# A hybrid decoder trunk: forgetting attention by two pairs of heads at a time, its gates' sums added on VectorE from a table that went through memory

## The chip, the core and the metric

The kernel runs on one core of a Trainium2 chip. A core has a matrix engine (TensorE, PE in the profile, with its weight loads PEld), a vector engine (VectorE, DVE), a scalar engine (ScalarE, ACT), GpSimd (POOL) and a queue that issues transfers (SyncE, SP). Each engine works through its own instructions in the order in which they were written, and waits there for semaphores of the others. The metric is the device time of one execution in microseconds: 1077.19 us before the change, the median of three runs (1077.06 to 1077.48).

## The reference

Two layers on 256 tokens of width 1024. Each is a half-step feed-forward block, a mixer, a second half-step feed-forward block and a gated input embedding, each followed by a layer norm. The first layer's mixer is forgetting attention (FoX) with 16 heads of 64; the second layer's is latent attention. Only the first mixer is touched by the change:

```python
def fox_mixer(x, w_in, b_f, w_o):
    h = x @ w_in
    q, k, v = ...                       # 16 heads of 64 each
    f_logit = h[..., 3 * D_MODEL:] + b_f
    cum = jnp.cumsum(jax.nn.log_sigmoid(f_logit), axis=1).transpose(0, 2, 1)
    scale = FOX_HEAD_DIM ** -0.5
    def scores(start):
        ...
        s = jnp.einsum('bqhd,bkhd->bhqk', qb, k) * scale
        return s + cb[:, :, :, None] - cum[:, :, None, :]
    o = causal_block_attention(scores, v)     # causal mask, softmax, times v
    return o.reshape(B, S, D_MODEL) @ w_o
```

So to the score of query t and key s comes the difference of two running sums of log gates, cum[t] - cum[s].

## The kernel before

All matrix products run on TensorE in a float32 form that wants each operand as a high part and a low part; a product is then three matmuls (high by high, high by low, low by high: `mm3`, or three terms written out). Making the parts is the steady work of two engines: ScalarE copies the high part (line 498 for a PSUM result, lines 193 and 201 for weights), and VectorE then subtracts it from the source and writes the low part (lines 499, 194 and 205). A weight arrives by a transfer into one of three buffers `raw` (1 MB, two units each) and is split into one of ten slots `hl` or a slot that is lent for a time (`fs`, `qk`, `ota`, `otb`). `Stream.pump` decides by planned times where a split is written between matmuls; with `S.hold` set it writes none, and `S.split_now()` (or `S.ahead()` for the high part and `S.later()` for the low one) puts one at a chosen place.

The FoX mixer handles 256 tokens, eight pairs of heads j = 0..7. First come the values and gate logits (`VA`, `VB`, `VC`). `gates()` turns the logits into running sums in small steps `s1`...`s6` that are dropped between matmuls; they end in a tile `m8`, minus eight times the sums, and in `negc`, its high and low parts in four blocks of partitions. Then each pair goes through these steps, whose short names the text keeps:

- K(j) and Q(j): `gen_k`, `gen_q`, 24 matmuls of 128x256 into one bank of the PSUM ring "h" (two banks, used in turn), then the two parts into `qk` (two buffers, by j % 2).
- QK(j): for both heads the scores of the causal blocks, 384 columns, into two banks of ring "y" (four banks). Two matmuls with `sel` and `negc` put -8 cum[s] there first, and twelve matmuls of 64 rows add q by k.
- softmax(j): on VectorE four fused operations (line 1028) add the causal mask and take the row extremes, two tiny operations per head subtract and add cum[t] (`tt`, lines 1035 and 1036); on ScalarE four exponentials with row sums (line 1040); VectorE takes reciprocals (line 1047), GpSimd divides (line 1050).
- T(j): six transposes on TensorE into the two banks of ring "tr", then the parts into `PT`.
- AV(j): six matmuls, into a bank of ring "y", then the parts into `ota` or `otb` (lines 1091 and 1094).
- O(k, t): the output projection of pair k for token half t, six matmuls of 128x512 that add into two banks of ring "y".

The loop of before overlaps neighbouring pairs: K(j+1), T(j-1), QK(j), softmax(j), Q(j+1), AV(j-1). At its end come the O steps, the layer norm `ln` of each token half, and the transposes XT of the normed half that the next feed-forward block needs.

## Time and profile before

| quantity | value |
|---|---|
| time, median of 3 runs | 1077.19 us (1077.06 to 1077.48) |
| profiled execution: its time, its span | 1080.02 us, 1077.9 us |
| granted TensorE clock | 0.997 of full speed |
| TensorE busy in the span | 1064.3 us, 99% |
| VectorE, ScalarE, GpSimd busy | 721.5 us, 543.8 us, 60.2 us |
| pairs 0 to 5 of the FoX loop (223.12 to 273.56 us), busy: TensorE, VectorE, ScalarE, GpSimd | 50.44 us of 50.44; 42.08; 35.30; 14.45 |
| K(0) begins; next feed-forward block begins | 212.84 us; 305.10 us |

The profile shows one execution. A row of its timeline gives the start and the duration in us, the engine, the line, the operation with output and inputs, and in brackets the idle time of the engine just before, with what ended it. TensorE's matmuls overlap, so the time that one costs is read from start to start. A count such as x24 says that a row merges so many like instructions.

### The profile page before, as it was taken

What the parts mean: (1) busy time and instruction counts of PE and PEld (TensorE: products, weight loads), DVE (VectorE), ACT (ScalarE), POOL (GpSimd) and SP (SyncE); (2) the same over time, 40 slices, a digit from 0 to 9 for tenths busy, and PEclk for the clock granted to TensorE, in tenths of its full rate; (3) what the DMA queues carried; (4) which work ended last, traced back from release to release, by engine and by line L of the source; (5) the groups of instructions that cost most, each with busy time, mean ns of one, the idle gap of its engine ahead of it and who ended that gap; (6) DMA issues with size and microseconds to landing.
All of it is one profiled execution on the core that took longest, in us unless ns stands there. A gap on an engine that the chain in (4) does not pass through costs nothing.

```text
span 1077.9 us, 17528 instructions
## 1 busy us (share of the span) xinstructions
PE 1064.3 (99%) x7236; PEld 974.0 (90%) x7236; DVE 721.5 (67%) x1053; ACT 543.8 (50%) x805; POOL 60.2 (6%) x94
## 2 busy tenths in 40 slices
PE   9999999999999999999999999999999999999997
PEld 8989998999889899998899999988889789898986
DVE  5675545788897545548966554389877886455566
ACT  5654433667655444444564443337666465344431
POOL 0000000223100000001320000010000000000000
PEclk9999999999999999999999999999999999999999
DMA  7885642543348655444477554334334568555502
GB/s 276 335 297 222 236 159 93 204 173 118 130 177 296 233 191 196 146 177 166 168 262 274 195 194 148 108 93 147 130 126 159 185 225 314 181 207 188 186 11 78
DMA packets 33092, 199.58 MB, mean 185 GB/s; under 512 B 3699, under 2 KB 5491, under 8 KB 12149
## 3 DMA queue, kind: packets, MB, share of 16 engines
q1 hardware_dynamic: 33012, 198.47, 51.5%
q8 instruction: 57, 0.93, 0.3%
q14 instruction: 23, 0.18, 0.1%
HBM read 197.40 MB, written 1.05 MB: 184 GB/s over the span
## 4 chain that ended last, share of the span: by engine, by line
PE 87%; DVE 8%; ACT 2%; issue 1%; POOL 1%; DMA 0%; DVEq 0%; SPq 0%; POOLq 0%; ACTq 0%
PE y L489 31%; PE h L489 31%; PE tr L489 22%; DVE hl L194 2%; PE tr L493 2%; ACT P L1425 1%; DVE x L569 1%; ACT hl L193 1%; DVE PT L499 1%; DVE tr L1420 0%; DVE st L551 0%; DVE x L550 0%; PE h L493 0%; DVE qk L499 0%; DVE hl L205 0%
## 5 line engine op out<-in xcount | busy, mean ns | idle before, releaser
L194 DVE TENSOR_TENSOR hl<-raw,hl 128x1024 fp32r<-128x1024 f32 (+3 forms) x267 | 312.8, 1191 | 149.5 <-ACT hl L193 148.3
L193 ACT ACTIVATE hl<-raw 128x1024 fp32r<-128x1024 f32 (+3 forms) x267 | 269.3, 1031 | 184.9 <-PE y L489 97.6
L489 PE MATMUL y<-hl,g 128*128 128x512 f32 x816 | 190.7, 390 | 0.0
L489 PE MATMUL h<-xT,hl 128*128 128x256 f32 x1560 | 188.0, 280 | 0.4 <-DVE hl L233 0.2
L489 PEld LDWEIGHTS h<-xT,hl 128*128 128x128 f32 x1560 | 183.4, 190 | 2.6 <-ACT xT L498 0.6
L489 PEld LDWEIGHTS y<-hl,g 128*128 128x128 f32 x816 | 152.0, 188 | 30.7
L489 PE MATMUL tr<-xT,hl 128*128 128x256 f32 x1512 | 176.6, 277 | 0.0
L489 PEld LDWEIGHTS tr<-xT,hl 128*128 128x128 f32 x1512 | 174.2, 188 | 0.5
L489 PE MATMUL h<-hl,xT 128*128 128x512 f32 (+2 forms) x300 | 67.8, 374 | 0.4 <-DVE xT L499 0.4
L489 PE MATMUL y<-hl,xT 128*128 128x512 f32 (+3 forms) x360 | 65.4, 334 | 0.0
L489 PEld LDWEIGHTS h<-hl,xT 128*128 128x128 f32 x300 | 53.2, 188 | 10.7 <-DVE xT L499 1.0
L489 PEld LDWEIGHTS y<-hl,xT 128*128 128x128 f32 x360 | 55.5, 188 | 6.3 <-ACT xT L498 0.4
L561 POOL TENSOR_TENSOR rs<-ve,mhalf 128x1 f32<-128x1 f32 x16 | 15.1, 943 | 633.7 <-DVE ve L560 633.7
L489 PE MATMUL y<-hl,otb 128*128 128x512 f32 x168 | 43.8, 402 | 1.2 <-DVE otb L499 1.0
L499 DVE TENSOR_TENSOR g<-P,g 128x512 fp32r<-128x512 f32 x38 | 26.3, 693 | 26.6 <-ACT g L498 26.6
L498 ACT ACTIVATE xT<-tr 128x512 fp32r<-128x512 f32 x28 | 16.1, 597 | 49.3 <-PE tr L493 49.3
L498 ACT ACTIVATE g<-P 128x512 fp32r<-128x512 f32 x38 | 24.1, 634 | 32.7 <-DVE P L678 32.7
L489 PEld LDWEIGHTS y<-hl,otb 128*128 128x128 f32 x168 | 30.6, 192 | 7.8 <-DVE otb L499 1.4
L194 DVE TENSOR_TENSOR otb<-raw,otb 128x1024 fp32r<-128x1024 f32 (+1 forms) x20 | 24.1, 1203 | 17.3 <-ACT otb L193 17.3
L194 DVE TENSOR_TENSOR qk<-raw,qk 128x1024 fp32r<-128x1024 f32 (+1 forms) x21 | 25.7, 1222 | 12.0 <-ACT qk L193 12.0
L677 ACT ACTIVATE P<-tr 128x512 f32<-128x512 f32 x20 | 12.0, 600 | 39.3 <-PE tr L489 39.3
L678 DVE TENSOR_TENSOR P<-P,tr 128x512 f32<-128x512 f32 x20 | 13.8, 688 | 25.0 <-PE tr L489 13.4
(264 smaller groups left out, 1411.1 us busy)
## 6 DMA issues: line engine op xcount, KB each, us to landing
raw<-in_ffn_in_dram SPq DMA_DIRECT2D x85, 1024.0 KB, 4.9
raw<-in_ffn_out_dram SPq DMA_DIRECT2D x44, 1024.0 KB, 5.0
raw<-in_pg_dram SPq DMA_DIRECT2D x8, 1024.0 KB, 4.8
raw<-in_mo_dram SPq DMA_DIRECT2D x8, 1024.0 KB, 4.7
raw<-in_kq_dram SPq DMA_DIRECT2D x8, 640.0 KB, 5.2
gb<-in_ln_g_dram SPq DMA_DIRECT2D x8, 512.0 KB, 5.8
gb<-in_ln_b_dram SPq DMA_DIRECT2D x8, 512.0 KB, 7.3
raw<-in_fk_dram SPq DMA_DIRECT2D x4, 1024.0 KB, 4.9
```

Source lines behind the costliest of these rows:

```text
L193: nc.scalar.activation(hi, src, AF.Copy)
L194: nc.vector.tensor_tensor(lo, src, hi.bitcast(F32), op=ALU.subtract)
L489: self.nc.tensor.matmul(out, lhsT, rhs, start=start, stop=stop)
L493: self.nc.tensor.transpose(out, in_, self.ident)
L498: self.nc.scalar.activation(hi, src, AF.Copy)
L499: self.nc.vector.tensor_tensor(lo, src, hi.bitcast(F32), op=ALU.subtract)
L561: nc.gpsimd.tensor_tensor(rs, ve, self.mhalf, op=ALU.pow)
L569: nc.vector.scalar_tensor_tensor(xs, xs, rs if i else mv[:, 0:1], self.gb[:, i, c0:c1], op0=ALU.mult if i else ALU.subtract, op1=ALU.add i ...
L677: nc.scalar.activation(gt, ps[0], AF.Silu)
L678: nc.vector.tensor_tensor(gt, gt, ps[1], op=ALU.mult)
L1425: nc.scalar.activation(P[:, c0:c1], b[:, c0:c1], AF.Exp, bias=nm[:, q : q + 1], scale=-1.0, accum_out=su[:, q : q + 1],)
```

## The change

The running sums no longer enter the scores through TensorE. `s4` writes the 16 rows of `m8` to a small tensor `fox_c` in memory; `decay_load(j)` reads the rows of the two heads of pair j back with two transfers that repeat them on all 128 partitions, into one of two halves of a tile `mb`; `decay_mask(j)` puts the causal mask into it with two operations on GpSimd. The fused VectorE operation of softmax(j) then adds `mb` in place of the mask, and the two matmuls with `sel` and `negc` are gone from QK. Three small steps of the gates move from GpSimd to VectorE. `mb` takes the buffer of the layer norm's gains `gb`, so the gains of the mixer's norm are loaded after softmax(7) instead of at j = 2.

The loop now runs over two pairs a, a+1: QK(a), QK(a+1), softmax(a), AV(a-1), K(a+2), softmax(a+1), Q(a+2), K(a+3), T(a), Q(a+3), AV(a), T(a+1). The divisions are steps of their own (`divide`), behind softmax(a+1) and behind K(a+3). `tt` is computed for both heads of a pair at once. Four weight splits per round are written at fixed places, and AV writes into ring "h" (AV(5) into "tr"). The O steps and the last pairs are in a new order.

```diff
         bf = self.tl([128, 1], F32, "bf", 1)
-        sel = self.tl([128, 16], F32R, "sel", 1)
-        negc = self.tl([128, 384], F32R, "negc", 1)
+        mb = self.tl([128, 2, 2, 384], F32, "gb", 1)
...
-        nc.gpsimd.memset(negc.bitcast(F32), 0.0)
-        sf = fs[:, 1792:1808]
-        nc.gpsimd.tensor_tensor(sf, self.ident[:, 16:32], self.ident[:, 48:64], op=ALU.add)
-        nc.gpsimd.tensor_tensor(sf, sf, self.ident[:, 80:96], op=ALU.add)
-        nc.gpsimd.tensor_tensor(sel, sf, self.ident[:, 112:128], op=ALU.add)
...
+
+        def decay_load(j):
+
+            if not self.rec:
+                o = mb[:, j % 2]
+                for c0, n in ((0, 128), (128, 256)):
+                    row = self.fox_c[2 * j, 0:1]
+                    src = bass.AP(tensor=row.tensor, offset=row.offset, ap=[[0, 128], [256, 2], [1, n]])
+                    nc.sync.dma_start(o[:, :, c0 : c0 + n], src)
+
+        def decay_mask(j):
+
+            for c0 in (0, 256):
+                o = mb[:, j % 2, :, c0 : c0 + 128]
+                nc.gpsimd.affine_select(
+                    out=o, in_=o, pattern=[[0, 2], [-1, 128]], compare_op=ALU.is_ge, fill=NEG,
+                    base=0, channel_multiplier=1,
+                )
 
         def gates():
             ps = self.bank("tr")
@@ -930,39 +942,31 @@
                 self.S.busy(act=2400)
                 nc.gpsimd.tensor_scalar(u, e, 1.0, 1.0, op0=ALU.add, op1=ALU.mult)
                 nc.gpsimd.tensor_scalar(r, u, -1.0, 1.0, op0=ALU.add, op1=ALU.mult)
-                nc.gpsimd.tensor_tensor(e, r, e, op=ALU.subtract)
+                nc.vector.tensor_tensor(e, r, e, op=ALU.subtract)
 
             def s2():
                 nc.scalar.activation(ab, u, AF.Ln)
                 self.ready_for(AF.Exp)
                 nc.vector.reciprocal(r, u)
-                nc.gpsimd.tensor_tensor(e, e, r, op=ALU.mult)
-                nc.gpsimd.tensor_tensor(u, e, ab, op=ALU.subtract)
+                nc.vector.tensor_tensor(e, e, r, op=ALU.mult)
                 nc.gpsimd.memset(r, 0.0)
                 self.S.busy(act=1600, dve=1600)
 
             def s3():
+                nc.vector.tensor_tensor(u, e, ab, op=ALU.subtract)
                 nc.vector.scalar_tensor_tensor(f, f, 0.0, u, op0=ALU.min, op1=ALU.add)
                 nc.vector.tensor_tensor_scan(sc[fr, :], f, r, 0.0, op0=ALU.add, op1=ALU.add)
                 nc.gpsimd.tensor_scalar(m8, sc[fr, :], -8.0, 1.0, op0=ALU.mult, op1=ALU.mult)
                 self.S.busy(dve=600)
 
             def s4():
-                nc.scalar.activation(negc[fr, 0:128], m8[:, 0:128], AF.Copy)
-                nc.scalar.activation(negc[fr, 128:384], m8, AF.Copy)
-
-            def s5():
-                nc.vector.tensor_tensor(
-                    negc[64:96, 128:384], m8, negc[fr, 128:384].bitcast(F32), op=ALU.subtract
-                )
-                nc.vector.tensor_copy(negc[64:96, 0:128], negc[64:96, 128:256].bitcast(F32))
-                self.S.busy(dve=400)
-
-            def s6():
-                nc.vector.tensor_copy(negc[0:64, :], negc[64:128, :].bitcast(F32))
+                self.dma(self.fox_c, m8[16:32, :])
+                for j in range(2):
+                    decay_load(j)
+                    decay_mask(j)
 
             rest = lambda: None
-            self.bg.extend((s1, rest, rest, s2, rest, rest, s3, rest, s4, s5, s6))
+            self.bg.extend((s1, rest, rest, s2, rest, s3, s4))
 
         def gates_transpose():
...
         def gen_k(j):
-            gen(j, "fk", 256, {0: S.split_now} if j >= 2 else {}, j >= 2)
+            gen(j, "fk", 256, {}, j >= 2)
...
@@ -1000,18 +1004,12 @@
             sb = [self.bank(ring) for _ in range(2)]
             half = [slice(0, 64), slice(64, 128)]
             o = qk[:, j % 2]
-            for s in range(2):
-                h = 2 * j + s
-                self.mm(
-                    sb[s][:, 0:384], sel[half[s], h : h + 1].to_broadcast([64, 128]), negc[half[s], :],
-                    True, False,
-                )
             for n, (i, jj) in enumerate(((0, 0), (0, 1), (1, 0))):
                 for q0, c0, c1 in ((0, 0, 128), (128, 128, 384)):
                     for s in range(2):
                         self.mm(
                             sb[s][:, c0:c1], o[half[s], i, q0 : q0 + 128],
-                            o[half[s], jj, 256 : 256 + c1 - c0], False, n == 2 and q0 > 0,
+                            o[half[s], jj, 256 : 256 + c1 - c0], n == 0 and q0 == 0, n == 2 and q0 > 0,
                         )
             st[j] = sb
...
@@ -1026,14 +1024,13 @@
             for s in range(2):
                 for q, (c0, c1) in enumerate(seg):
                     nc.vector.tensor_tensor_reduce(
-                        out=sb[s][:, c0:c1], in0=sb[s][:, c0:c1], in1=self.mask[:, c0:c1],
+                        out=sb[s][:, c0:c1], in0=sb[s][:, c0:c1], in1=mb[:, j % 2, s, c0:c1],
                         op0=ALU.add, op1=ALU.min, scale=-0.125, scalar=3.0e38,
                         accum_out=nm[:, 2 * s + q : 2 * s + q + 1],
                     )
-                c2 = cq[:, 2 * j + s, :]
-                i = slice(2 * s, 2 * s + 2)
-                nc.vector.tensor_tensor(tt[:, i], nm[:, i], c2, op=ALU.subtract)
-                nc.vector.tensor_tensor(tt[:, i], tt[:, i], c2, op=ALU.add)
+            c2 = cq[:, 2 * j : 2 * j + 2, :].rearrange("p h t -> p (h t)")
+            nc.vector.tensor_tensor(tt, nm, c2, op=ALU.subtract)
+            nc.vector.tensor_tensor(tt, tt, c2, op=ALU.add)
             for s in range(2):
                 for q, (c0, c1) in enumerate(seg):
                     i = 2 * s + q
@@ -1043,17 +1040,17 @@
                     )
             self.S.busy(act=1800, dve=1400)
 
-            def divide(s):
-                nc.vector.reciprocal(su[:, 2 * s : 2 * s + 2], su[:, 2 * s : 2 * s + 2])
-                for q, (c0, c1) in enumerate(seg):
+            st[j] = P, su
+
+        def divide(j):
+            P, su = st[j]
+            nc.vector.reciprocal(su, su)
+            for s in range(2):
+                for q, (c0, c1) in enumerate(((0, 128), (128, 384))):
                     i = 2 * s + q
                     nc.gpsimd.tensor_scalar(
                         P[s][:, c0:c1], P[s][:, c0:c1], su[:, i : i + 1], 1.0, op0=ALU.mult, op1=ALU.mult
                     )
-
-            divide(0)
-            divide(1)
-            S.later()
             st[j] = P
...
-        def AV(j):
+        def AV(j, what=None):
             o = PT.pop(j)
-            ps = self.bank("y" if j < 6 else "tr")
+            ps = self.bank("h" if j != 5 else "tr")
             n, c = j // 4, 128 * (j % 4)
...
+            if what:
+                what()
             ot = OT[j // 4][:, j % 4]
...
-        for j in range(8):
-            if j == 2:
-                self.load_gb(li, 1)
-            S.hold = j >= 1
-            if j < 7:
-                gen_k(j + 1)
-            else:
-                O(0, 0)
-                O(1, 0)
-            if j == 0:
-                self.flush()
-                gates_transpose()
-                S.lend("fs")
-            if j >= 1:
-                T(j - 1)
-                if j < 7:
-                    S.ahead()
-            QK(j, "y" if j < 7 else "h")
-            softmax(j)
-            if j < 7:
-                gen_q(j + 1)
-            else:
-                O(2, 0)
-                S.split_now()
-                O(3, 0)
-            if j >= 1:
-                AV(j - 1)
+        gen_k(1)
+        gen_q(1)
+        self.flush()
+        gates_transpose()
+        S.lend("fs")
+        S.hold = True
+        for a in range(0, 8, 2):
+            QK(a, "y")
+            QK(a + 1, "y" if a < 6 else "h")
+            softmax(a)
+            if a:
+                AV(a - 1)
+            if a == 6:
+                break
+            decay_load(a + 2)
+            gen_k(a + 2)
+            softmax(a + 1)
+            decay_load(a + 3)
+            divide(a)
+            S.split_now()
+            gen_q(a + 2)
+            S.split_now()
+            gen_k(a + 3)
+            divide(a + 1)
+            decay_mask(a + 2)
+            decay_mask(a + 3)
+            T(a)
+            S.split_now()
+            gen_q(a + 3)
+            S.split_now()
+            AV(a, lambda: T(a + 1))
+        S.lend("qk")
+        O(0, 0)
+        softmax(7)
+        self.load_gb(li, 1)
+        divide(6)
+        S.split_now()
+        O(1, 0)
+        S.split_now()
+        O(2, 0)
+        divide(7)
         S.hold = False
-        S.lend("qk")
+        O(3, 0)
         O(4, 0)
+        T(6)
         O(5, 0)
+        AV(6)
         T(7)
+        O(0, 1)
+        O(1, 1)
+        AV(7)
         O(6, 0)
-        O(0, 1)
-        AV(7)
-        O(1, 1)
+        O(2, 1)
         O(7, 0)
         self.ln(0, y[0], ALPHA, LN_EPS)
-        for k in range(2, 8):
+        for k in range(3, 8):
             O(k, 1)
         self.ln(1, y[1], ALPHA, LN_EPS)
...
+    dr = ctx.enter_context(tc.tile_pool(name="dr", bufs=1, space=bass.MemoryType.DRAM))
...
+    Trunk(nc, (sb, ps), a, S, False, dr.tile([16, 256], F32, name="fox_c")).run()
```

On ScalarE the row of work around softmax(2) and softmax(3) stood before like this (`P` are the exponentials, `qk` the parts of K or Q, `ota` those of AV, `PT` those of T, `hl` a weight split):

```order
L1040 ACTIVATE P,su<-y,tt 128x256
L498 ACTIVATE qk<-h 128x256
L1091 ACTIVATE ota<-y 64x256 x2
L201 ACTIVATE hl_2580<-raw 128x1024
L498 ACTIVATE qk<-h 128x256
L498 ACTIVATE PT<-tr 128x512
L498 ACTIVATE PT<-tr 128x256
L201 ACTIVATE hl_2624<-raw 128x1024
L1040 ACTIVATE P,su<-y,tt 128x128
```

and stands now like this:

```order
L1037 ACTIVATE P,su<-y,tt 128x256
L1090 ACTIVATE ota<-h 64x256 x2
L498 ACTIVATE qk<-h 128x256
L1037 ACTIVATE P,su<-y,tt 128x128
L1037 ACTIVATE P,su<-y,tt 128x256
L1037 ACTIVATE P,su<-y,tt 128x128
L1037 ACTIVATE P,su<-y,tt 128x256
L201 ACTIVATE hl_2651<-raw 128x1024
L498 ACTIVATE qk<-h 128x256
L201 ACTIVATE hl_2681<-raw 128x1024
```

The splits that stood between two groups of exponentials now stand behind the second group.

On VectorE, behind the row extremes of softmax(2), stood before (`su` the reciprocals, `y,nm<-y,mask` the fused operation of the next pair):

```order
L1036 TENSOR_TENSOR tt<-tt,cq 128x2
L1047 RECIPROCAL su<-su 128x2 x2
L205 TENSOR_TENSOR hl_2500<-raw,hl_2500 128x1024
L499 TENSOR_TENSOR qk<-h,qk 128x256
L1094 TENSOR_TENSOR ota<-y,ota 64x256 x2
L205 TENSOR_TENSOR hl_2580<-raw,hl_2580 128x1024
L499 TENSOR_TENSOR qk<-h,qk 128x256
L499 TENSOR_TENSOR PT<-tr,PT 128x512
L499 TENSOR_TENSOR PT<-tr,PT 128x256
L1028 ISA y,nm<-y,mask 128x128
```

and stands now, up to the fused operation of softmax(3):

```order
L1032 TENSOR_TENSOR tt<-nm,cq 128x4
L1033 TENSOR_TENSOR tt<-tt,cq 128x4
L1093 TENSOR_TENSOR ota<-h,ota 64x256 x2
L499 TENSOR_TENSOR qk<-h,qk 128x256
L1026 ISA y,nm<-y,gb 128x128
```

Between the two softmaxes of a round VectorE has only the low parts of AV(a-1) and K(a+2).

At the end of the mixer, ScalarE's row behind the exponentials of softmax(7) was before (`otb` the parts of AV(6) and AV(7)):

```order
L1040 ACTIVATE P,su<-h,tt 128x256
L201 ACTIVATE hl_3146<-raw 128x1024
L1091 ACTIVATE otb<-tr 64x256 x2
L193 ACTIVATE hl_3168<-raw 128x1024
L193 ACTIVATE fs<-raw 128x1024
L498 ACTIVATE PT<-tr 128x512
```

and is now:

```order
L1037 ACTIVATE P,su<-h,tt 128x256
L201 ACTIVATE fs<-raw 128x1024
L201 ACTIVATE hl_3148<-raw 128x1024
L193 ACTIVATE hl_3164<-raw 128x1024
L193 ACTIVATE qk<-raw 128x1024
L498 ACTIVATE PT<-tr 128x512
L498 ACTIVATE PT<-tr 128x256
L1090 ACTIVATE otb<-h 64x256 x2
```

The parts of T(6) come behind four splits, and T(7), AV(6) and AV(7) behind them.

5 lines of the change are left out of this document (2 added, 3 removed).

## The prediction

> **What bounds the kernel now.** I read the page first (busy shares, then the chain), then the timeline of each engine over one period of the loop, QK(5) to QK(6).
>
> ```profile
> span 1077.9 us, 17528 instructions
> PE 1064.3 (99%) x7236; PEld 974.0 (90%) x7236; DVE 721.5 (67%) x1053; ACT 543.8 (50%) x805; POOL 60.2 (6%) x94
> PE 87%; DVE 8%; ACT 2%; issue 1%; POOL 1%; DMA 0%; DVEq 0%; SPq 0%; POOLq 0%; ACTq 0%
> ```
>
> TensorE is busy for 99% of the span and holds 87% of the chain. So a microsecond of matmul taken away counts, as long as TensorE never has to wait. One period on TensorE:
>
> ```profile
> 262.75 0.60 PE L1065 MATMUL tr<-ident,P 128*128 128x128 f32 x4
> ...
> 263.50 0.44 PE L489 MATMUL y<-negc,sel 64*128 64x384 f32 x2
> 263.78 0.85 PE L489 MATMUL y<-qk 64*128 64x128 f32 x12
> 264.56 3.01 PE L489 MATMUL h<-xT,hl 128*128 128x256 f32 x24
> 267.41 1.21 PE L489 MATMUL y<-PT,g 128*128 128x512 f32 x6
> 268.46 3.00 PE L489 MATMUL h<-xT,fs 128*128 128x256 f32 x24
> ```
>
> From start to start: T 0.75, the gate matmuls 0.28, QK 0.78, Q or K 2.85, AV 1.05; the period is 8.54 and no row shows idle time. The same period on VectorE and ScalarE:
>
> ```profile
> 265.02 0.29 DVE L1028 CUSTOM_DVE_ANT_0 y<-y,mask 128x128 f32<-128x128 f32 x1
> ...
> 265.93 0.16 DVE L1035 TENSOR_TENSOR tt<-nm,cq 128x2 f32<-128x2 f32 x1
> ...
> 266.20 0.29 DVE L1028 CUSTOM_DVE_ANT_0 y<-y,mask 128x128 f32<-128x128 f32 x1
> ...
> 267.31 0.16 DVE L1036 TENSOR_TENSOR tt<-tt,cq 128x2 f32<-128x2 f32 x1
> 267.42 0.17 DVE L1047 RECIPROCAL su<-su 128x2 f32<-128x2 f32 x1
> 268.51 0.17 DVE L1047 RECIPROCAL su<-su 128x2 f32<-128x2 f32 x1 [0.93 <-ACT P L1040]
> 268.59 1.20 DVE L205 TENSOR_TENSOR hl<-raw,hl 128x1024 fp32r<-128x1024 f32 x1
> 269.72 0.42 DVE L499 TENSOR_TENSOR qk<-h,qk 128x256 fp32r<-128x256 f32 x1
> 270.05 0.85 DVE L1094 TENSOR_TENSOR otb<-y,otb 64x256 fp32r<-64x256 f32 x2
> ...
> 272.62 1.02 DVE L499 TENSOR_TENSOR PT<-tr,PT 128x512 fp32r<-128x512 f32 x2
> 273.56 0.29 DVE L1028 CUSTOM_DVE_ANT_0 y<-y,mask 128x128 f32<-128x128 f32 x1
> ```
>
> ```profile
> 267.56 0.37 ACT L1040 ACTIVATE P<-y,tt 128x128 f32<-128x128 f32 x1 [0.25 <-DVE tt L1036]
> ...
> 268.37 0.39 ACT L498 ACTIVATE qk<-h 128x256 fp32r<-128x256 f32 x1
> 268.66 0.78 ACT L1091 ACTIVATE otb<-y 64x256 fp32r<-64x256 f32 x2
> 269.46 1.06 ACT L201 ACTIVATE hl<-raw 128x1024 fp32r<-128x1024 f32 x1
> 271.49 0.38 ACT L498 ACTIVATE qk<-h 128x256 fp32r<-128x256 f32 x1 [0.97 <-PE h L489]
> 271.99 0.87 ACT L498 ACTIVATE PT<-tr 128x512 fp32r<-128x512 f32 x2
> ```
>
> VectorE, too, needs 8.54 from one softmax to the next (265.02 to 273.56), of which it waits 0.93 for an exponential. It is hardly freer than TensorE: it keeps up because the low part of a split, whose high part ScalarE made earlier, fills the time of the exponentials. Prices from these rows: softmax on VectorE 2.40, of it 0.27 for a head's two tiny operations; split low 1.13, Q or K low 0.33, both T lows 0.94, both AV lows 0.85. On ScalarE: one head's exponentials 0.81, starting 0.25 behind the last tiny operation; AV highs 0.80, Q or K high 0.38, split high 1.06; a Q or K high can start 3.03 after that step began on TensorE (268.46 to 271.49). A low starts about 0.03 behind its high.
>
> **Removed on TensorE.** Eight times 0.28 is 2.24 us, the only gain on the bounding engine. [...]
>
> **The new round on VectorE and ScalarE.** softmax(a) takes 2.40 - 0.27 = 2.13 on VectorE, and its exponentials start 2.27 after its first fused operation (267.31 - 265.02 - 0.27 + 0.25). But VectorE's next work is the low parts of AV(a-1) and K(a+2), whose highs stand on ScalarE behind all four exponentials. So, from the first operation of softmax(a): exponentials to 2.27 + 1.62 = 3.89, AV highs to 4.69, VectorE's two lows to 5.15, K low to 5.48. Only then comes softmax(a+1); its exponentials end at 5.48 + 3.89 = 9.37, the first split's high at 10.43, and VectorE goes on at 10.46. What follows is four split lows (4.52), three Q or K lows (0.99), two T pairs (1.88), AV (0.85), two reciprocals (0.1): 8.34. One wait of 0.6 lies in it: Q(a+3) needs the bank that Q(a+2)'s low frees at 12.1, its high starts at 15.1, and the last split's high comes behind it, to 16.5. With about 0.1 for GpSimd's divisions ahead of T(a+1) the round takes 19.5. TensorE's own work in it is 2 x (0.78 + 1.05 + 0.75) + 4 x 2.85 = 16.56; two old periods were 17.08. So the loop changes its bound: VectorE and ScalarE take turns instead of overlapping.
>
> TensorE's waits follow. AV(a-1) now has a bank of ring "h", so Q(a+2), two users on, cannot begin before AV(a-1)'s lows at 5.2; TensorE is there at 3.2 and waits 2.0. Q(a+3) waits 0.5 and T(a+1) 0.5 (next paragraph). That is 3.0 in each of the rounds a = 2 and 4: 6.0. Round 0 has no AV(a-1); the same sums give 1.4 at Q(3) and 0.5 at T(1): 1.9.
>
> **GpSimd.** Its divisions follow a reciprocal by 0.1:
>
> ```profile
> 267.68 0.83 POOL L1050 TENSOR_SCALAR P<-P,su 128x128 f32<-128x128 f32 x2 [5.72 <-DVE su L1047]
> 268.77 1.73 POOL L1050 TENSOR_SCALAR P<-P,su 128x128 f32<-128x128 f32 x2 [0.27 <-DVE su L1047]
> ```
>
> Two take 0.83 while VectorE waits and 1.73 beside a split. divide(a+1) now lies beside lows, between 1.7 and 3.4 for its four; at about 2.8 T(a+1) is 0.5 late. The masks come behind: a select has 256 columns against the 384 of such a pair, so 0.6 to 1.2 each by these rows, two per pair; they end about a microsecond before the softmax that reads them and cost nothing while that cover holds.
>
> **The table through memory.** The sums are ready where they were, and then take a store, a load and a mask:
>
> ```profile
> bf<-in_fox_b_f_dram SPq DMA_DIRECT2D x1, 0.1 KB, 1.5
> fs<-in_xt_dram SPq DMA_DIRECT2D x2, 128.0 KB, 2.3
> nrm<-in_kv_norm_dram SPq DMA_DIRECT2D x1, 128.0 KB, 6.4
> ```
>
> ```profile
> 215.25 1.80 POOL L940 TENSOR_TENSOR fs<-fs 32x256 f32<-32x256 f32 x1
> 217.08 0.42 DVE L945 SCALAR_TENSOR_TENSOR fs<-fs 32x256 f32<-32x256 f32 x1
> 218.38 0.41 POOL L947 TENSOR_SCALAR fs<-fs 32x256 f32<-32x256 f32 x1 [1.08 <-DVE fs L946]
> ```
>
> ```profile
> 218.80 3.01 PE h L489 x24
> ```
>
> Before, `m8` is done at 218.79. The moved steps cost VectorE 0.42 each instead of GpSimd 1.80; the last now stands in VectorE's queue ahead of K(0)'s low part, which releases K(1) at 218.80, so both `m8` and K(1) come about 0.3 later. K(1), Q(1), the transposes and QK(0) on TensorE then put softmax(0) at 226.1. Bounds for the table: store 1.5 and load 2.3 as at the quiet rows, or a load of 6.4 as for the repeated row that came beside other traffic; with 0.5 for the second transfer's issue and 0.6 to 1.2 for its mask, ready between 224.1 and 228.9. No weight load stands ahead of it, so I take the low end, which is hidden; the other end delays softmax(0) by 2.8. The four transfers and the store also hold up one weight load on SP by some 4 us; three loads are in flight ahead of need, so nothing. The later loads wait on SP for softmax(a), and the norm's gains for softmax(7), 17 us ahead of their use.
>
> **The end of the mixer.**
>
> ```profile
> 297.32 0.69 DVE L550 SCALAR_TENSOR_TENSOR x<-x,y 128x512 f32<-128x512 f32 x1
> ...
> 303.04 0.75 DVE L569 SCALAR_TENSOR_TENSOR x<-x,rs,gb 128x512 f32<-128x512 f32 x1
> ```
>
> ```profile
> 298.72 4.25 PE L489 MATMUL y<-hl,otb 128*128 128x512 f32 x18
> 302.80 0.60 PE L493 MATMUL tr<-ident,x 128*128 128x128 f32 x4
> ...
> 305.10 1.22 PE L489 MATMUL h<-hl,xT 128*128 128x512 f32 x4
> ```
>
> An O step takes 1.36 (three from 298.72 to 302.80). From the first operation of softmax(6): QK(7)'s second bank is AV(4)'s, freed only at 0.1, and TensorE waits 1.6. softmax(7) on VectorE stands behind AV(5)'s lows, so its exponentials end at 9.1, and T(6), behind divide(6), waits 0.5. On ScalarE four split highs now stand ahead of T(6)'s parts, and on VectorE four lows, from 10.2 to 14.8; the low that AV(6) needs ends at 15.5. TensorE reaches AV(6) at 11.4, behind only one O step, and waits 3.9. The layer norm (6.47 from 297.32 to its last piece) has four O steps as cover now instead of five: 0.3.
>
> **The sum.** Waits 0.6 at K(1), 1.9, 6.0, 1.6 + 0.5 + 3.9 + 0.3: 14.8. Of the 92.26 from 212.84 to 305.10, matmul steps explain 91.3, so 1.0 of waits was there before. 14.8 - 1.0 - 2.2 = +11.6. On the profiled execution that is a span of 1089.5 and a time of 1091.6; its 1080.02 stands 2.83 above the median, so the median goes to 1088.8.
>
> **Rivals.** *The end absorbs its waits*: the four splits turn out to run before the last exponentials' turn, so that T(6) and AV(6) are on time. For it: before, the same kind of splits fit there; against it: the order on ScalarE. It gives 11.6 - 4.4 = +7.2, 1084.4. *The table is late*: the load of 6.4 above, +14.4, 1091.6; the loop is bound by VectorE from softmax(0) on, so nothing takes it back. *TensorE stays the bound* (the other side): the round's own VectorE work is 4.26 + 4.52 + 1.32 + 1.88 + 1.7 + 0.1 = 13.8, and if its waits stay under 3.3 of the 5.7 that I count, a round is no longer than 17.08; if TensorE then never waits, the gain is the whole 2.2, 1075.0. For it: VectorE waited only 0.93 per period. Against it: each of the two waits per round is an exponential group plus a high part, 2.7 by rows, with nothing ahead of it in VectorE's queue.
>
> **Numbers.** My forecast 0.66, the absorbing end 0.12, the late table 0.12, TensorE as bound 0.10. The range reaches from below the absorbing end to beyond the late table, 1081.0 to 1092.5, and leaves out the last case. About 0.2% is what a measurement tells from no change: faster 0.09, within 0.01, slower 0.90.
>
> **What would show it.** In the profile after: no gate matmuls; a round of about 19.5 between softmax(2), softmax(4) and softmax(6); VectorE idle for some 2 us, released by ScalarE, twice a round; TensorE idle ahead of Q(4) and Q(6) by about 2, QK(7) 1.6, AV(6) some 4; softmax(0) released by TensorE and not by a mask. I am wrong if VectorE's idle time per round stays below 3, if the masks release the softmaxes, or if the four splits do not stand in AV(6)'s way.

## The result, and the profile after

The changed kernel takes 1094.15 us (median of six runs, 1092.55 to 1096.68) against 1077.34 for the kernel before on the same chip (six runs): a ratio of 1.0151, 95% interval 1.0138 to 1.0165. Forecast were 1088.8, with a range of 1081.0 to 1092.5. The direction was right, the size was 5.4 us too small and the time lies above the range.

The head, the chain's line and TensorE's waits from the page and the list of waits of the changed kernel (in the list: microseconds in all, how often, the longest):

```profile
span 1094.7 us, 17543 instructions
...
PE 1068.2 (98%) x7220; PEld 976.5 (89%) x7220; DVE 717.8 (66%) x1029; ACT 541.7 (49%) x803; POOL 63.5 (6%) x103
...
PE 62%; DVE 8%; ACT 2%; issue 1%; POOL 0%; DVEq 0%; POOLq 0%; ACTq 0%
```

```profile
PE h L489 <- DVE ota L1093: 5.2, 2, 2.6
PE h L489 <- DVE qk L499: 2.6, 3, 1.6
PE h L489 <- DVE otb L1093: 1.9, 1, 1.9
PE h L489 <- DVE PT L499: 1.9, 2, 1.5
...
PE h L489 <- ACT PT L498: 1.2, 1, 1.2
PE tr L493 <- DVE x L569: 1.0, 2, 0.8
```

TensorE's share of the chain falls from 87% to 62%. Two things in these rows don't fit together at first sight. The waits stand where they were forecast. But TensorE's busy time *rose*, from 1064.3 to 1068.2, although eight pairs of gate matmuls are gone.

The comparison is cleanest over the stretch that the change rewrites, from the first matmul of K(0) to the first of the next feed-forward block. One row of the busy times of that stretch, of the kernel before and of the changed one (its numbers: the length, the busy time of TensorE, of its weight loads, of VectorE, ScalarE and GpSimd, each with its instructions in brackets, and then the granted clock, third from the end):

```profile
212.84:305.10 92.26, 91.93 (x700) 83.55 (x698) 77.20 (x202) 59.55 (x143) 22.86 (x37) 1.00 0.42 149
```

```profile
213.51:323.37 109.86, 96.55 (x683) 86.68 (x682) 75.09 (x178) 57.36 (x141) 28.86 (x51) 0.94 0.45 154
```

The stretch went from 92.26 to 109.86, +17.6 (forecast +11.6). TensorE idles 13.3 in it where it idled 0.3, and is busy 4.6 longer where 2.24 less was expected: 6.9 of the loss is the same work done more slowly. The granted clock says how: 0.94 over the stretch. In pieces of 3.41 us:

```profile
246.80:250.22 3.42, 1.77 (x16) 1.57 (x14) 0.86 (x5) 2.42 (x11) 0.00 (x0) 1.00 0.61 208
250.22:253.63 3.41, 2.46 (x21) 2.49 (x22) 3.12 (x14) 0.32 (x2) 0.00 (x0) 1.00 0.20 36
267.28:270.70 3.42, 1.27 (x12) 1.07 (x10) 0.87 (x4) 2.74 (x11) 0.00 (x0) 1.00 0.50 169
270.70:274.11 3.41, 2.96 (x14) 2.99 (x15) 2.63 (x13) 0.51 (x3) 0.32 (x1) 0.50 0.08 25
284.35:287.76 3.41, 1.54 (x14) 1.35 (x15) 3.18 (x12) 0.34 (x1) 0.29 (x1) 1.00 0.67 211
287.76:291.18 3.42, 3.42 (x12) 2.73 (x11) 0.86 (x5) 2.35 (x10) 0.00 (x0) 0.50 0.24 98
298.00:301.42 3.42, 1.32 (x5) 0.55 (x3) 3.42 (x5) 2.24 (x4) 2.10 (x1) 1.00 0.38 97
301.42:304.83 3.41, 2.80 (x12) 2.61 (x12) 0.99 (x3) 0.81 (x3) 1.36 (x4) 0.50 1.01 423
304.83:308.24 3.41, 3.41 (x10) 2.73 (x9) 1.76 (x4) 1.30 (x3) 0.00 (x0) 0.50 0.25 103
```

Four such windows, and no other in the stretch, ran at half clock. They hold 2.96 + 3.42 + 2.80 + 3.41 = 12.6 of TensorE's work. In the last of them work took twice as long: the two O steps that begin at 304.82 took 4.43 and not 2.72, 1.71 more, with 3.42 of it at half clock. By that, as an estimate, half of the 12.6, 6.3 of the 6.9, is what the half clock cost in work. This execution has the lowest mean clock of the six, 0.992; the other five have 0.994 or 0.995 and so lose less in this way. Each run of slow windows begins behind one in which TensorE was busy for 1.54 or less of 3.41. One row shows it in an instruction group; Q(6) is 24 matmuls that take 2.85 elsewhere:

```profile
271.15 4.37 PE L489 MATMUL h<-xT,fs 128*128 128x256 f32 x24 [2.60 <-DVE ota L1093]
275.36 2.88 PE L489 MATMUL h<-xT,hl 128*128 128x256 f32 x24
```

The first wait of a round, softmax(2), in the timeline of VectorE, ScalarE and TensorE:

```profile
245.47 0.30 DVE L1026 CUSTOM_DVE_ANT_0 y<-y,gb 128x128 f32<-128x128 f32 x1
...
247.77 0.37 ACT L1037 ACTIVATE P<-y,tt 128x128 f32<-128x128 f32 x1 [3.52 <-DVE tt L1033]
...
249.37 0.77 ACT L1090 ACTIVATE ota<-h 64x256 fp32r<-64x256 f32 x2
250.16 0.38 ACT L498 ACTIVATE qk<-h 128x256 fp32r<-128x256 f32 x1
250.16 0.86 DVE L1093 TENSOR_TENSOR ota<-h,ota 64x256 fp32r<-64x256 f32 x2 [2.49 <-ACT ota L1090]
251.05 0.42 DVE L499 TENSOR_TENSOR qk<-h,qk 128x256 fp32r<-128x256 f32 x1
...
251.40 0.29 DVE L1026 CUSTOM_DVE_ANT_0 y<-y,gb 128x128 f32<-128x128 f32 x1
```

This is the picture of the prediction: the exponentials end at 249.37, 3.90 behind the first fused operation (forecast 3.89), the AV highs follow, VectorE has waited 2.49 for them, and Q(4) on TensorE waits 2.60 for the AV lows. One size is off: the lows start when *both* highs are done (250.16), not behind the first, so softmax(3) starts 5.93 behind softmax(2) and not 5.48.

The stretch by its parts, from the start of K(0) over the first fused operations of softmax(0), (2), (4) and (6) to the next block, in microseconds of each profiled execution; the line "forecast" is worked out from the prediction's numbers (226.1 - 212.84; 16.56 + 1.9; 19.5 twice; the rest of 92.26 + 11.6):

| | to softmax(0) | (0) to (2) | (2) to (4) | (4) to (6) | to the next block | sum |
|---|---|---|---|---|---|---|
| before | 10.28 | 16.28 | 17.08 | 17.08 | 31.54 | 92.26 |
| forecast | 13.26 | 18.46 | 19.5 | 19.5 | 33.1 | 103.9 |
| changed | 13.35 | 18.61 | 19.98 | 20.65 | 37.27 | 109.86 |
| e8_again, the same kernel | 13.36 | 18.51 | 20.86 | 21.01 | 35.85 | 109.59 |
| e1_fill | 13.56 | 18.46 | 19.95 | 19.93 | 34.37 | 106.27 |
| e7_fill_tr | 13.36 | 18.51 | 19.94 | 19.91 | 34.40 | 106.12 |
| e2_table | 10.26 | 25.20 | 16.97 | 17.20 | 30.82 | 100.45 |
| e5_table2 | 10.46 | 16.45 | 17.23 | 17.23 | 30.71 | 92.08 |
| e3_pairs | 13.28 | 18.42 | 19.65 | 19.64 | 35.82 | 106.81 |
| e4_av_first | 13.36 | 19.09 | 18.68 | 18.64 | 32.79 | 102.56 |
| e6_ahead | 13.37 | 16.97 | 17.40 | 16.83 | 33.54 | 98.11 |
| e9_best | 12.92 | 16.30 | 16.65 | 16.37 | 28.91 | 91.15 |

### The profile page after: what moved, and what is told of

Same layout as the page of the kernel before. It is cut to its first block, busy times and chain, and to the rows that moved or that the text cites. A ratio compares the mean times of both kernels' runs of the same rounds, so it can differ in the third digit from the quotient of the medians.

```text
span 1094.7 us, 17543 instructions
## 1 busy us (share of the span) xinstructions
PE 1068.2 (98%) x7220; PEld 976.5 (89%) x7220; DVE 717.8 (66%) x1029; ACT 541.7 (49%) x803; POOL 63.5 (6%) x103
## 3 DMA queue, kind: packets, MB, share of 16 engines
HBM read 200.55 MB, written 1.06 MB: 184 GB/s over the span
## 4 chain that ended last, share of the span: by engine, by line
PE 62%; DVE 8%; ACT 2%; issue 1%; POOL 0%; DVEq 0%; POOLq 0%; ACTq 0%
PE y L489 23%; PE h L489 20%; PE tr L489 17%; DVE hl L194 2%; PE tr L493 1%; ACT P L1441 1%; DVE x L569 1%; DVE st L551 1%; DVE x L550 1%; ACT hl L193 0%; DVE tr L1436 0%; DVE hl L205 0%; DVE PT L499 0%; POOL rs L561 0%; DVE qk L194 0%
## 5 line engine op out<-in xcount | busy, mean ns | idle before, releaser
L489 PE MATMUL y<-hl,g 128*128 128x512 f32 x804 | 187.3, 390 | 0.0
L205 DVE TENSOR_TENSOR hl<-raw,hl 128x1024 fp32r<-128x1024 f32 (+1 forms) x24 | 29.1, 1214 | 9.7 <-ACT hl L201 9.7
```

Of the source, the lines that this page charges most:

```text
L205: nc.vector.tensor_tensor(lo, src, hi.bitcast(F32), op=ALU.subtract)
L489: self.nc.tensor.matmul(out, lhsT, rhs, start=start, stop=stop)
```

## The experiments

The chips of the experiments ran the kernel before in 1079.05, 1078.51 and 1078.76 (medians), so that ratios to the kernel before on the same chip are compared, and the stretch of the table, which leaves out what differs between executions ahead of the change and behind it.

### e1_fill and e7_fill_tr: TensorE's waits filled with work that nobody reads

```diff
+    def fill(self, out, n):
+        for _ in range(n):
+            self.nc.tensor.matmul(out, self.ident, self.mask, start=True, stop=True)
...
+            if a:
+                self.fill(self.bank("tr")[:, 0:384], 4)
             gen_q(a + 2)
...
+            if j == 7:
+                self.fill(sb[0][:, 0:384], 3)
...
+            if j == 6:
+                self.fill(ps[:, 0:384], 5)
```

> The changed kernel with matmuls added that nobody reads: four of 128x384 in f32 ahead of Q(4) and of Q(6), three ahead of QK(7), five ahead of AV(6), all where TensorE waits in the changed kernel. Theory 'the clock follows TensorE's waits': in the profiled run of the changed kernel the granted clock stood at 0.50 in 270.7 to 274.1, 287.7 to 291.1 and 301.4 to 308.3 us, each time behind a wait, and nowhere else in the loop. With the waits filled it stays at 1.00 from 250 to 310 us, the profiled span comes down from 1094.7 by 5 to 6 us although TensorE has about 9 us more to do, and the median from 1094.2 to about 1091. Theory 'the slow matmuls have another cause' (transfers that run beside them, or the kind of matmul): the clock drops at the same places, the median stays at 1094 or rises by up to 2 where a filler delays a real step.

Measured: 1091.23, ratio 1.0118 (1.0104 to 1.0131), span 1089.3. The clock in the busy times by stretch of e1_fill, the places that were slow among them:

```profile
260.00:270.00 10.00, 10.00 (x76) 8.01 (x75) 6.67 (x21) 4.83 (x16) 2.95 (x6) 1.00 0.57 205
270.00:280.00 10.00, 9.78 (x81) 9.41 (x81) 7.10 (x18) 6.68 (x17) 3.79 (x8) 1.00 0.31 88
280.00:290.00 10.00, 10.00 (x62) 7.51 (x62) 6.52 (x21) 4.40 (x15) 2.87 (x5) 1.00 0.43 163
...
300.00:310.00 10.00, 10.00 (x52) 8.45 (x51) 6.20 (x9) 5.57 (x9) 0.30 (x1) 1.00 0.44 154
```

The first theory holds for the clock: it stays at 1.00 in the whole stretch, the mean clock is 0.998 in all four executions where the changed kernel has 0.992 to 0.995, and the stretch falls from 109.86 to 106.27. Adding matmuls made the kernel faster. But of the 5.4 that the span is shorter 1.8 lies ahead of the change, where the fillers do nothing (K(0) starts at 211.72 and not at 213.51; the last section tells of such differences), so that it was partly luck that the span came out as forecast. The stretch falls by 3.6 and not by the 6.3 of slowed work, since part of that work ran where TensorE would otherwise have waited: round (4) to (6) is 0.7 shorter, the end 2.9.

The same with transposes as fillers:

```diff
-        for _ in range(n):
-            self.nc.tensor.matmul(out, self.ident, self.mask, start=True, stop=True)
+        for _ in range(4 * n):
+            self.nc.tensor.transpose(out[:, 0:128], self.ident, self.ident)
```

> e1_fill with transposes in place of its matmuls as fillers, four 128x128 for each matmul. Theory 'any work of TensorE keeps the clock': as e1_fill, granted clock 1.00 from 250 to 310 us and a ratio of about 1.012. Theory 'transposes do not count as work for the clock': windows of 3.4 us at 0.50 as in the changed kernel, and a ratio of 1.014 to 1.017.

Measured: 1094.24, ratio 1.0148 (1.0134 to 1.0162). The two signs disagree. In the profiled execution the clock is 1.00 from 250 to 310 and the stretch is 106.12, as with e1_fill. By its timeline's rows, no window of 3.41, wherever its edges lie, has TensorE busy for less than 1.84 when the filler transposes are counted. When they are not, every placing of the edges leaves a window of 1.0 or less, and such windows were followed by one at half clock in the other profiles (last section). So in this execution transposes counted as work. The mean clock of the four executions is 0.998, 0.998, 0.996 and 0.995, which points to windows at half clock in two of them, where e1_fill has 0.998 four times; these fillers are shorter (1.91 for sixteen ahead of Q(4) against 2.74 for e1_fill's) and leave a wait of 0.76. The rest of the difference in time lies ahead of the change: K(0) starts at 214.60 in this profile and at 211.72 in e1_fill's, and 2.5 of that is the stretch from 28 us on, 186.7 against 184.2 (last section). Whether the other three executions had it too is not shown.

### e8_again: the changed kernel once more

The kernel is unedited.

> The changed kernel unaltered, on the chip of the runs beside it. Theory 'the clock looks at fixed windows that do not follow the kernel': the waits stand where they were, within 0.1, but the windows at half clock stand at other places or are more or fewer, and the profiled span differs by about half a window's length, 1.7, for each. Theory 'the slow places belong to the kernel': the same steps are slow again, Q(6), the steps after QK(7) and T(7) to AV(7).

Measured: 1097.51, ratio 1.0174 (1.0161 to 1.0188).

```profile
250.28:253.69 3.41, 0.82 (x7) 0.75 (x7) 1.55 (x6) 2.02 (x9) 0.00 (x0) 1.00 0.44 100
253.69:257.11 3.42, 3.42 (x18) 3.42 (x18) 1.63 (x9) 1.68 (x9) 1.49 (x4) 0.50 0.15 46
270.76:274.17 3.41, 0.91 (x8) 0.73 (x8) 1.30 (x4) 2.40 (x11) 0.00 (x0) 1.00 0.34 110
274.17:277.59 3.42, 3.42 (x19) 3.42 (x18) 1.88 (x11) 1.30 (x7) 1.11 (x3) 0.50 0.10 30
```

The waits ahead of Q(4) and Q(6) are the same (2.59 and 2.50 against 2.60 twice), but here Q(4) is slow as well as Q(6), and nothing is slow behind QK(7): the windows do not follow the kernel. Ahead of AV(6) TensorE waits 2.25 first and not 1.18, since the O steps before it ran at full clock. Both rounds are now over 20.8 where e1_fill has 19.95 and 19.93. So a wait of 2.6 can cost nothing more (246.80 to 253.63 of the first profile) or another 0.9 to 1.1 in its round, by where the window's edge falls in it. That the span would differ by 1.7 for each window was wrong: three windows and not four, and a span 1.6 *longer*; the stretch is 0.3 shorter, and K(0) starts 1.9 later.

### e2_table and e5_table2: the table without the pairing

The kernel before's loop, with the gates' sums of pairs 2 to 7 added on VectorE from the table; pairs 0 and 1 keep their gate matmuls.

```diff
-            for s in range(2):
+            for s in range(2 if j < 2 else 0):
                 h = 2 * j + s
...
-                        out=sb[s][:, c0:c1], in0=sb[s][:, c0:c1], in1=self.mask[:, c0:c1],
+                        out=sb[s][:, c0:c1], in0=sb[s][:, c0:c1], in1=self.mask[:, c0:c1] if j < 2 else mb[:, j % 2, s, c0:c1],
...
             softmax(j)
+            if 2 <= j < 6:
+                decay_load(j + 2)
+            if 3 <= j < 7:
+                decay_mask(j + 1)
...
```

> The kernel before, its loop unchanged by one pair, with the table alone: pairs 2 to 7 get their gates' sums on VectorE from the table in memory, pairs 0 and 1 keep the gate matmuls. Theory 'the table costs nothing by itself and the pairing carries the loss': 6 x 0.28 = 1.7 us are taken from TensorE, the period goes from 8.54 to 8.26, the median from 1077.3 to about 1075.6. Rival 'VectorE and ScalarE bind the old loop too': the period stays at 8.54 and the time within 0.3 of before. Rival 'the masks on GpSimd or the loads come late': softmaxes released by a mask, periods of 9 and more, the time 1 to 4 above before.

Measured: 1086.04, ratio 1.0071 (1.0058 to 1.0085): none of the three. The last rival named the right engine and the wrong victim; from GpSimd's and TensorE's timeline:

```profile
232.46 0.41 POOL L935 TENSOR_SCALAR_AFFINE_SELECT gb<-gb 128x256 f32<-128x256 f32 x1 [2.42 <-DMA gb<-fox_c]
232.85 1.63 POOL L1073 TENSOR_SCALAR P<-P,su 128x128 f32<-128x128 f32 x4
...
233.28 1.74 PE L1088 MATMUL tr<-ident,P 128*128 128x128 f32 x4 [5.61 <-POOL P L1073]
```

The selects of pairs 2 and 3 had been put ahead of the divisions of pair 0 and waited there for their loads, which began at 224.02 and came in until 232.46. Nobody needed those masks yet, but the divisions behind them made T(0) wait 5.61, and two windows at half clock followed. e5_table2 has them behind the divisions:

```diff
                 for j in (2, 3):
                     decay_load(j)
-                    decay_mask(j)
...
-            if 3 <= j < 7:
+            if 1 <= j < 7:
                 decay_mask(j + 1)
```

> The table alone in the kernel before's loop once more, with the two first selects put behind a pair's divisions on GpSimd instead of ahead of them (in e2_table they waited there for their loads, and the first transposes stood 5.6 behind them). Theory 'the table costs nothing by itself': the 5.6 and the window at half clock behind it are gone, and each of the pairs 2 to 7 saves what e2_table's later periods showed, 8.54 - 8.35 = 0.19 and not 0.28 (QK alone took 0.90 there, the gate pair and QK 1.06 before); 6 x 0.19 = 1.1 below before. Rival 'the selects press on VectorE': the periods of the pairs 2 to 7 reach 8.5 again, the time within 0.5 of before or above it.

Measured: 1079.04, ratio 1.0004 (0.9994 to 1.0015), the stretch 92.08 against 92.26. The rival is right about the time. TensorE's steps of a pair follow each other by 8.35 (T(1) at 238.53, T(5) at 271.95), 0.19 less than before, but VectorE's own period is now 8.62:

```profile
249.40 0.29 DVE L1050 CUSTOM_DVE_ANT_0 y<-y,gb 128x128 f32<-128x128 f32 x1
...
258.02 0.29 DVE L1050 CUSTOM_DVE_ANT_0 y<-y,gb 128x128 f32<-128x128 f32 x1
```

Two places in VectorE's row have grown. The split low that follows a pair's selects takes 1.40 from start to start (246.73 to 248.13) where it took 1.26 before, and in each softmax that reads the table the second fused operation starts 0.48 behind the first and not 0.38. Only the first of them lies beside the selects, what makes the second is not shown, and smaller gaps elsewhere take up 0.16 of the two. VectorE falls behind TensorE by 0.27 a pair, and at the end of the loop the transposes are late (T(6) takes 1.10 from start to start and not 0.75). So by itself the table is worth nothing in the old loop: it takes 0.19 a pair from TensorE and puts about 0.1 on VectorE, which was as tight. And the gate matmuls' price in the prediction, 0.28, was too high for that loop: without them in front, QK takes 0.88 to 0.90 and not 0.78.

### e3_pairs: the pairing without the table

```diff
+            for s in range(2):
+                h = 2 * j + s
+                self.mm(
+                    sb[s][:, 0:384], sel[half[s], h : h + 1].to_broadcast([64, 128]), negc[half[s], :],
+                    True, False,
+                )
...
-                        out=sb[s][:, c0:c1], in0=sb[s][:, c0:c1], in1=mb[:, j % 2, s, c0:c1],
+                        out=sb[s][:, c0:c1], in0=sb[s][:, c0:c1], in1=self.mask[:, c0:c1],
...
-            decay_load(a + 2)
...
-            decay_load(a + 3)
...
-            decay_mask(a + 2)
-            decay_mask(a + 3)
```

> The changed kernel with the gate matmuls put back and the table taken out: the pairing of heads alone. Theory 'VectorE and ScalarE set the round': softmax(4) follows the lows of AV(2) with no wait of VectorE's, so the gate matmuls, 0.56 a round, lie in TensorE's waits; rounds 2 to 4 and 4 to 6 stay at about 20, and the median at 1093.5 to 1095.5. Rival 'the table carries a part of the loss': 1088 to 1091. Rival 'TensorE sets the round after all': the eight gate pairs come on top, 1096.5.

Measured: 1092.54, ratio 1.0126 (1.0112 to 1.0139). The time lies below the first theory's range, and on the first chip's 1077.34 it is 1090.9, just inside the first rival's. The rounds tell the parts:

```profile
244.85 0.30 DVE L1028 CUSTOM_DVE_ANT_0 y<-y,mask 128x128 f32<-128x128 f32 x1
...
264.50 0.30 DVE L1028 CUSTOM_DVE_ANT_0 y<-y,mask 128x128 f32<-128x128 f32 x1
```

19.65 and 19.64, with the gate matmuls in them, against 19.95 and 19.93 with the table and a full clock (e1_fill). So the pairing carries most of the loss; the gate matmuls lie in TensorE's waits, where taking them away saves nothing, and the table costs VectorE 0.3 a round. This profile has one window at half clock in the stretch and the changed kernel's has four, to which most of the rest of the 3.0 between them belongs: 0.7 in round (4) to (6), 1.4 at the end.

The same profile prices the gate matmuls where two QKs stand side by side:

```profile
242.23 0.45 PE L489 MATMUL y<-negc,sel 64*128 64x384 f32 x2
242.51 0.85 PE L489 MATMUL y<-qk 64*128 64x128 f32 x12
243.20 0.34 PE L489 MATMUL y<-negc,sel 64*128 64x384 f32 x2
243.38 0.85 PE L489 MATMUL y<-qk 64*128 64x128 f32 x12
244.16 1.32 PE L489 MATMUL h<-PT,g 128*128 128x512 f32 x6
```

The first two take 0.28 from start to start and the second two 0.18, and all four rows 1.93. Without them the changed kernel's two QKs take 1.58 (242.84 to 244.42), so a pair of gate matmuls costs 0.17 here. The other 0.1 of the 0.28 fell here on the matmuls of 64 rows that came first behind those of 128: in e5_table2 that is QK, with 0.89 instead of 0.78.

### e4_av_first and e6_ahead: the order on ScalarE's queue

```diff
-        def softmax(j):
+        def softmax(j, what=None):
...
             nc.vector.tensor_tensor(tt, tt, c2, op=ALU.add)
+            if what:
+                what()
...
-            softmax(a)
-            if a:
-                AV(a - 1)
+            softmax(a, (lambda: AV(a - 1)) if a else None)
```

> The changed kernel with one thing moved: the copies of AV(a-1) stand ahead of the exponentials of softmax(a) on ScalarE, and its lows directly behind the tiny operations of softmax(a) on VectorE, not behind all four exponentials. Theory 'the queue order on ScalarE makes the waits': VectorE has the AV lows as work during the exponentials, softmax(3), (5) and (7) start 1.3 earlier than in the changed kernel, the wait of 2.6 ahead of Q(4) and of Q(6) goes to 0 to 0.3, rounds 2 to 4 and 4 to 6 go from 20.0 and 20.6 to about 18.7; with fewer windows at half clock the median is 1088 to 1090.5. Rival 'the round is bound by the amount of work on VectorE and ScalarE, whatever its order': rounds stay at 19.5 or more, the median above 1092.5.

Measured: 1088.26, ratio 1.0085 (1.0072 to 1.0099); rounds of 18.68 and 18.64. The first theory holds to a tenth: the same work in another order on two queues takes 1.3 off each of these rounds, and the waits ahead of Q(4) and Q(6) are gone. Round (0) to (2), which has no AV of an earlier pair, is 0.5 longer.

In e6_ahead, S.ahead() writes the high part of the next split and S.later() its low part:

```diff
+            def mid():
+                if a:
+                    AV(a - 1)
+                S.ahead()
+            softmax(a, mid)
+            S.later()
...
-            softmax(a + 1)
+            softmax(a + 1, S.ahead)
...
-            S.split_now()
+            S.later()
             gen_q(a + 2)
...
-            S.split_now()
-            AV(a, lambda: T(a + 1))
+            if a < 4:
+                AV(a, lambda: T(a + 1))
+            else:
+                AV(a)
+                T(a + 1)
```

> e4_av_first with three more moves: the high part of a weight split stands ahead of the exponentials of softmax(a) and of softmax(a+1) on ScalarE, its low part on VectorE right behind that softmax's tiny operations (two splits a round that stood behind the exponentials), and AV(4)'s copies stand ahead of those of T(5). Theory 'the round is long because VectorE has no work during the exponentials': VectorE's waits of 2.7 and 1.3 a round fall below 0.5 each, the rounds go from 18.7 to 16.6 to 17.1, TensorE's waits ahead of Q(3), Q(5), Q(7) and QK(7) (1.5 to 1.8 each in e4_av_first) go, and the ratio to before falls from 1.0085 to 1.000 to 1.003. Rival 'the amount of work on VectorE binds': rounds of 18 and more, a ratio above 1.006.

Measured: 1083.76, ratio 1.0048 (1.0033 to 1.0063), rounds of 17.40 and 16.83: the direction of the first theory, short of its numbers. TensorE's waits ahead of Q(3), Q(5), Q(7) and QK(7) are gone, and of VectorE's in round (2) to (4) 0.92, 0.52 and 1.41 are left; but the next in line shows:

```profile
252.44 1.18 PE L1064 MATMUL tr<-ident,P 128*128 128x128 f32 x4
253.46 0.38 PE L493 MATMUL tr<-ident,P 128*128 128x128 f32 x2
253.59 2.98 PE L489 MATMUL h<-xT,hl 128*128 128x256 f32 x24
...
291.47 1.86 PE L489 MATMUL h<-PT,g 128*128 128x512 f32 x5 [1.32 <-DVE PT L499]
```

T(2) takes 1.15 from start to start and not 0.75: its transposes wait one by one for GpSimd's divisions, which started late and ran beside a split's low part. At the end AV(6) waits 1.33 and 1.32, and a last window at half clock follows.

### e9_best: the divisions where their exponentials end

```diff
             gen_k(a + 2)
+            divide(a)
             softmax(a + 1, S.ahead)
             decay_load(a + 3)
-            divide(a)
             S.later()
             gen_q(a + 2)
+            divide(a + 1)
             S.split_now()
             gen_k(a + 3)
-            divide(a + 1)
...
-        softmax(7)
-        self.load_gb(li, 1)
-        divide(6)
-        S.split_now()
+        divide(6)
+        softmax(7, S.ahead)
+        S.later()
+        self.load_gb(li, 1)
         O(1, 0)
-        S.split_now()
...
         T(6)
+        S.hold = False
```

Besides, the three gate steps that the change moved to VectorE are back on GpSimd.

> e6_ahead with what its rows still showed as waits moved: the divisions of a pair stand on VectorE's and GpSimd's queues as soon as that pair's exponentials end (in e6_ahead T(2) and T(3) took 1.15 from start to start and not 0.75, since the divisions ran beside split lows); the steps of the gates' chain that the change moved to VectorE are back on GpSimd (K(1) waited 0.57 for K(0)'s low behind them); at the end no further split stands ahead of T(6)'s parts (AV(6) waited 1.33 + 1.32). Theory 'only the order was wrong, the pairing and the table together save the gate matmuls': rounds fall from 17.4 to 16.6 to 16.8, the stretch from K(0) to the next block from 98.1 to 91.5 to 93 (before: 92.3), no window at half clock, a ratio of 0.998 to 1.001. Rival 'GpSimd and VectorE press on each other whatever the order': T stays at 1.0 or more, rounds at 17.2 or more, a ratio above 1.002.

Measured: 1077.51 (twelve runs) against 1078.76 (seventeen), ratio 0.9987, 95% interval 0.9976 to 0.9997: faster than the kernel before too, if only by 0.13% and with an interval that ends just short of 1.

```profile
241.11 0.30 DVE L1026 CUSTOM_DVE_ANT_0 y<-y,gb 128x128 f32<-128x128 f32 x1
...
257.76 0.30 DVE L1026 CUSTOM_DVE_ANT_0 y<-y,gb 128x128 f32<-128x128 f32 x1
```

```profile
PE 87%; DVE 8%; ACT 2%; issue 1%; POOL 1%; DMA 0%; SPq 0%; DVEq 0%; POOLq 0%; ACTq 0%
```

```profile
211.89:303.04 91.15, 89.71 (x683) 81.88 (x682) 74.49 (x176) 57.60 (x142) 29.49 (x53) 1.00 0.53 186
```

The round is 16.65 and then 16.37, about TensorE's own work; T is back at 0.75, no window is slow, and the chain is TensorE's again. TensorE is busy 89.71 of the stretch: 91.93 less 2.24 is 89.69, so in this order the whole sum that was forecast comes off, 1.4 of it for the gate matmuls and 0.8 because two QKs stand side by side (e3_pairs). What remains are waits of 0.31 ahead of K(1), 0.24 at QK(7) and 0.76 ahead of the layer norm's transposes.

## Why the prediction was right in sign and too small

**The gate matmuls, 2.24:** the sum came out (89.71 in e9_best), but by luck. Taking them away saves 0.17 a pair in the new loop, 1.4 in all, and 0.19 a pair in the old one. The other 0.8 is the pairing's: two QKs side by side, with the gate matmuls, take 1.93 and not 2 x 1.06. So the row's 0.28 from start to start was too high a price in both loops.

**The table hidden:** right. softmax(0)'s first fused operation was released by TensorE and its second waited 0.28 for a mask; 13.35 to softmax(0) where 13.26 was forecast. That the table costs nothing else was wrong by 0.3 a round (e3_pairs).

**Waits in K(1) and round 0:** right. K(1) waited 0.76 (0.6 forecast), round 0 took 18.61 (18.46).

**The round of 19.5:** the mechanism was right, as e4_av_first and e6_ahead show by taking it apart. Its size was 0.45 too small each time: "AV highs to 4.69, VectorE's two lows to 5.15" lets the lows start 0.03 behind their highs, and they wait for both. Without the table (e3_pairs) the first half of the round takes 5.84, 0.36 more than forecast, and the second 13.81, 0.2 less than forecast; the table's 0.3 comes on top.

**TensorE's waits, 14.8:** right in sum, to 1.7. The 1.0 that the sum takes off for waits of before was too much, since TensorE idles 0.3 there; with that, the sum would have come to +12.3. TensorE idles 13.3 in the stretch; with the clock held up, fillers and waits together are 106.2 - 89.7 = 16.5. At the end AV(6) waits 1.18 + 1.52 in the changed kernel and not 3.9, because the slow O steps ahead of it ran in that time; in e7_fill_tr, where nothing is slow, TensorE would be at AV(6) at 297.83, and its second matmul starts at 302.24.

**The step that failed is the one that adds waits to an unchanged sum of work:** "TensorE's own work in it is 16.56", with K or Q at 2.85 and O at 1.36. Those prices come from a kernel whose TensorE waits for 0.3 in this stretch. They were read at a granted clock of 1.00, and the prediction puts nothing in its sum for a lower one. In the changed kernel the waits leave TensorE 1.27, 1.54 and 1.32 of work in three windows of 3.41 us, and the work behind each of them runs at a granted clock of 0.50: Q(6) took 4.2 from start to start, and the two O steps behind T(7) took 4.43 (304.82 to 309.25) and not 2.72. Of the 6.0 us that the stretch is longer than forecast (109.86 against 103.9), 3.6 go when the clock is held up with fillers. The 2.4 that are left are the two rounds (0.45 and 0.43), the end (34.4 against 33.1) and 0.3 ahead of softmax(0).

The prediction has no rival on the clock at all: it counts its waits, 2.0 ahead of Q(4) and Q(6) and 1.6 at QK(7) among them, by their own length. In the runs single waits of 1.74 (e4_av_first, QK(7)) to 2.6 were enough for a window at half clock behind them, in windows that were busy for up to 1.68 of 3.41.

**The rivals:** none came. The end did not absorb its waits, the table was not late, and TensorE did not stay the bound; the last is what the same two ideas give in e9_best's order, 1.1 us of the 2.2 that the rival would have paid.

## What to carry to other kernels

A wait on a TensorE that was always busy can cost more than its length, by where it falls: a wait of 2.6 cost nothing more here or another 0.9 to 1.1. So look at the granted clock in windows of a few microseconds behind it, and price the steps that follow by both clocks. Where two engines hand work back and forth, the order on each queue made the time here, more than the amount: all but the same instructions took 109.9 and 91.2 (three small steps of the gates changed their engine). And a group of matmuls that is removed is worth the time by which the work behind it comes earlier, and not its own time from start to start: 0.17 to 0.19 of 0.28 here.

## What the runs showed of the hardware

*Slow work came in pieces of 3.41.* In this stretch of all profiled executions with slow work in it, the pieces at a granted clock of 0.50 last 3.41 or a multiple (twice 3.41 in the changed kernel and in e2_table). Where an execution has several, their edges lie on one grid of 3.41, wherever the kernel's steps lie: in the changed kernel they begin at 270.70, 287.76 and 301.42, which is 5 and then 4 windows on, and in e8_again at 253.69, 274.17 and 304.89, which is 6 and then 9. Around the slow windows of the six profiles that have them (the changed kernel, e8_again, e2_table, e3_pairs, e4_av_first and e6_ahead), a window at full clock with TensorE busy 1.68 or less of 3.41 was followed by one at half clock, and one with 1.77 or more was not. The row that came nearest, of e4_av_first:

```profile
281.45:284.86 3.41, 1.68 (x17) 1.33 (x16) 3.18 (x12) 0.57 (x2) 1.06 (x3) 1.00 0.68 211
284.86:288.28 3.42, 3.42 (x11) 2.82 (x10) 1.77 (x9) 2.21 (x9) 0.00 (x0) 0.50 0.24 98
```

A slow window that was itself not full was followed by another when it was busy for 2.77 (e2_table) or 2.80 (the changed kernel, at 301.42), and by one at full clock when it was busy for 2.96 (the changed kernel, at 270.70) or more. Transposes counted as work in e7_fill_tr's profile: its clock is 1.00 from 250 to 310, where without the filler transposes a window would have been busy for 1.0 or less. The lower mean clock of two other executions, 0.996 and 0.995, is not explained, so that this stays open.

*The same matmuls took 2.72 or 2.83 at full clock.* Ahead of the changed code, a group of 24 matmuls of 256 columns takes 2.72 in some stretches and 2.83 in others, at a granted clock of 1.00, and which stretch has which differs between executions of one kernel: from 28 us on to K(0) the changed kernel took 185.5 in one profile and 186.7 in the other, and the kernel before 184.2; e1_fill took 184.2 and e7_fill_tr 186.7. That alone moves the time by up to 2.5 us and is nothing of the change; no run here tells what sets it.
